# One matmul adds masks and the negative maximum to attention scores, in place of a second query tile and selects on GpSimd

## The chip, the cores and the metric

The kernel runs on one core of a Trainium2 chip. The metric is the device time of one execution in microseconds (us). The runs of the kernel before give 1493.66, 1497.61 and 1716.20 us; the median is 1497.61 us.

## The reference

Two layers of a decoder trunk are computed for a prompt of 1024 tokens and for 8 samples of 4 new tokens each, which share the weights. Layer 0 is attention: one input projection gives queries, keys and values for type A (a window of 128, with a sink logit in the denominator) and for three dilated groups of type B, 8 query heads over 2 key heads of width 64 each; then a gate, an output projection and a layer norm. Layer 1 is an mLSTM. The change touches the prompt's attention in layer 0, whose core is this (queries in blocks of 128 read their own and the block of keys before):

```python
def banded_attention(q, k, v, span, sink=None):
    ...
    s = jnp.einsum('nbqhgd,nbkhd->nbhgqk', qb, kk, preferred_element_type=F32)
    dist = qi - ki
    band = (dist >= 0) & (dist <= span)
    ...
    p, den, lse = _softmax_stats(s, mask, sink_b)
    o = jnp.einsum('nbhgqk,nbkhd->nbqhgd', p, vv.astype(F32))

def _softmax_stats(s, mask, sink):
    s = jnp.where(mask, s, NEG_INF)
    m = s.max(-1)
    ...
    p = jnp.exp(s - m[..., None])
    den = p.sum(-1)
```

The samples attend to their caches of 128, 128, 512 and 2048 rows (the last two strided, 128 rows of each taken).

## The kernel before

Layer 0 projects keys and values (`proj_kv`), then queries of four groups (`proj_q`, g = 0 for type A, 1 to 3 for type B with strides 1, 4, 16) and the gate (`proj_z0`), all through weights split into a high and a low part. Queries, keys and values go to DRAM scratch (QQ, KK, VV) and come back per group and key head (`kv`).

Attention has two passes. `stats` finds each query's maximum with masked scores in the layout queries x keys; `neg_rows` turns the maxima into rows of -maximum and stores them as a 129th row of QQ. `scores` (line 450) then computes the scores again in the layout keys x queries, for 4 heads x 128 queries at a time: a query block (`qb`). A query block has one score block (own keys) or two (the block before as well), as `blocks` says: 15 for each kv in groups 0 and 1, 12 in group 2, 8 in group 3, 100 in all. A score block is

- two matmuls into a PSUM tile `sc`: K1 (high keys twice, 128 rows) times Q1 (high and low queries), and K2 (low keys and a row of ones, 65 rows) times Q2 (high queries and the row of -maximum),
- `p = exp(sc)` on ScalarE (L465),
- the mask: selects on GpSimd that write zeros into `p` (L468 to L476),
- `ph`, `p` rounded, on ScalarE (`hi`, L112), and `pl = p - ph` on VectorE (`lo`, L116), or on GpSimd for every fourth block of type B (L481),
- three matmuls of `ph`, `ph` and `pl` with the values into `av` (L485 to L487), which VectorE adds to the outputs OD (L578, L580).

`q2_load` (line 364) makes Q2 for two query blocks at a time: one DMA of the -maximum row (1 partition x 4 x 256) and a copy of Q1's high half on ScalarE (L370). `k_load` makes K1 and K2, with a memset of the row of ones.

The order of the work is set in two steps. `weave` interleaves streams by planned costs: type A and the statistics of groups 1 and 2 with the projections of queries; then the statistics of group 3 and the scores of groups 3, 2, 1 for kv = 0, and the start of those for kv = 1, with the gate projections; then the rest of kv = 1 (`self.late`), the attention of the samples (`sample_attn`) and merges into the mixed activations (`merge0`). The framework's scheduler then puts every engine's instructions into one order by a model of their times, and each engine runs its own in that order. Nearly all DMAs are issued by SyncE (`load`, L106, and `store`, L109), in order too.

`sample_attn` loads the caches' keys and values into tiles KT (`sample_keys`, from a pool `smt` of 4 buffers that is opened after the pool `sm` is released at line 970), multiplies them (sS at L681, so at L728), and is followed in `out0` by the output projection (py, L165 to L167), whose weights (wr <- in_wo0) come through two buffers.

## Time and profile before

| | |
|---|---|
| median of the runs | 1497.61 us |
| profiled execution | 1500.81 us |
| its span, first to last instruction | 1499.1 us |
| mean granted clock of TensorE | 0.973 |
| TensorE busy (matmul) | 1405.4 us, 94% |
| VectorE busy | 901.5 us, 60% |
| ScalarE busy | 515.1 us, 34% |
| GpSimd busy | 276.0 us, 18% |

The profile is of one execution. Its engines are PE (TensorE matmul), PEld (its weight loads), DVE (VectorE), ACT (ScalarE), POOL (GpSimd) and SP (SyncE, which issues DMAs); an L number is a line of the kernel. Busy shares are means over stages with different limits, so a stage is read by its own stretch of time. Type A's scores run from 192 to 345 us, those of groups 3, 2 and 1 from 467 to 636 us, layer 0's output projection to 800 us, and layer 1 after that.

### The profile page before, as it was taken

The numbers are of one execution on the slowest core, as the hardware profiler recorded it, in microseconds if no ns is written. First come the engines' busy times: TensorE is split into PE (matmuls) and PEld (weight loads), VectorE is DVE, ScalarE is ACT, GpSimd is POOL, SyncE is SP. The second block draws the span as 40 slices with busy tenths as digits, with TensorE's granted clock in tenths as the row PEclk, the third lists the DMA queues.
The fourth block names the chain that finished last, engine by engine and source line by source line (L and its number), as shares of the span: only waits on it lengthen the run. The fifth ranks groups of instructions, "written<-read, shape, count | busy, mean of one in ns | idle before, by whom it ended". The sixth has DMA issues, their size and how long they took to land.

```text
span 1499.1 us, 21984 instructions
## 1 busy us (share of the span) xinstructions
PE 1405.4 (94%) x7792; PEld 1191.7 (79%) x7792; DVE 901.5 (60%) x2479; ACT 515.1 (34%) x938; POOL 276.0 (18%) x351
## 2 busy tenths in 40 slices
PE   8999999998899778979999999999999999999997
PEld 7989999898898444458788878988898899877785
DVE  5411457578566858768764536655565565566786
ACT  5332244542123776621133313331333133333310
POOL 1002233422322866401000000100000000000010
PEclk9999999999999888989999999999999999999999
DMA  8445655556653766794212655354223312431731
GB/s 307 168 142 171 199 190 164 173 162 185 186 190 111 195 169 186 241 300 140 95 51 87 220 191 201 109 194 124 78 82 122 108 50 69 131 116 39 233 131 46
DMA packets 139307, 226.86 MB, mean 151 GB/s; under 512 B 17216, under 2 KB 107296, under 8 KB 138680
## 3 DMA queue, kind: packets, MB, share of 16 engines
q1 hardware_dynamic: 131134, 204.09, 44.5%
q10 hardware_dynamic: 8064, 21.37, 4.0%
q8 instruction: 62, 1.02, 0.3%
q14 instruction: 47, 0.39, 0.1%
HBM read 166.60 MB, written 81.88 MB: 166 GB/s over the span
## 4 chain that ended last, share of the span: by engine, by line
PE 69%; DMA 16%; DVE 8%; issue 3%; ACT 2%; POOL 2%; SPq 1%; DVEq 0%; ACTq 0%; POOLq 0%
PE pj L199 10%; PE pj L201 10%; PE pj L200 10%; PE py L165 4%; PE py L167 3%; PE py L166 3%; DMA G<-GR 3%; PE pvo L165 3%; PE pvo L166 3%; PE pvo L167 3%; DMA wr<-in_wo_dram 1%; PE st L433 1%; DMA QZ<-QQ 1%; DMA out_cmems_dram<-Cs 1%; PE sc L463 1%
## 5 line engine op out<-in xcount | busy, mean ns | idle before, releaser
L199 PE MATMUL pj<-xh,wh 128*128 128x384 f32 (+1 forms) x576 | 189.3, 329 | 8.1 <-DVE sz L613 3.6
L199 PE MATMUL pj<-x1h,wh 128*128 128x384 f32 (+1 forms) x576 | 189.5, 329 | 1.7 <-ACT QT L1152 1.6
L200 PE MATMUL pj<-xl,wh 128*128 128x384 f32 (+1 forms) x576 | 188.5, 327 | 0.0
L201 PE MATMUL pj<-xh,wl 128*128 128x384 f32 (+1 forms) x576 | 188.4, 327 | 0.0
L201 PE MATMUL pj<-x1h,wl 128*128 128x384 f32 (+1 forms) x576 | 187.6, 326 | 0.0
L200 PE MATMUL pj<-x1l,wh 128*128 128x384 f32 (+1 forms) x576 | 187.4, 325 | 0.0
L199 PEld LDWEIGHTS pj<-xh,wh 128*128 128x128 f32 x576 | 110.6, 192 | 12.7 <-DVE sz L613 4.5
L199 PEld LDWEIGHTS pj<-x1h,wh 128*128 128x128 f32 x576 | 108.5, 188 | 6.5 <-issue 3.3
L201 PEld LDWEIGHTS pj<-x1h,wl 128*128 128x128 f32 x576 | 108.4, 188 | 6.0 <-issue 5.8
L200 PEld LDWEIGHTS pj<-xl,wh 128*128 128x128 f32 x576 | 110.5, 192 | 1.6
L201 PEld LDWEIGHTS pj<-xh,wl 128*128 128x128 f32 x576 | 110.8, 192 | 1.1
L200 PEld LDWEIGHTS pj<-x1l,wh 128*128 128x128 f32 x576 | 108.5, 188 | 4.0 <-issue 3.8
L437 DVE CUSTOM_DVE_ANT_0 junk<-st,maskq 128x256 f32<-128x256 f32 (+1 forms) x256 | 93.1, 364 | 27.4 <-PE st L433 6.8
L165 PE MATMUL pvo<-voh,x1h 128*128 128x512 f32 x256 | 101.0, 397 | 2.6 <-DVE SZ L1168 2.6
L166 PE MATMUL pvo<-voh,x1l 128*128 128x512 f32 x256 | 100.3, 394 | 0.0
L167 PE MATMUL pvo<-vol,x1h 128*128 128x512 f32 x256 | 99.7, 393 | 0.0
L807 POOL TENSOR_TENSOR rsw<-rsw,mhalf 128x1 f32<-128x1 f32 (+1 forms) x54 | 40.0, 741 | 322.3 <-DVE rsw L806 306.6
L116 DVE TENSOR_TENSOR pl<-p,ph 128x512 fp32r<-128x512 f32 x82 | 67.0, 825 | 29.0 <-ACT ph L112 27.0
L122 POOL TENSOR_TENSOR wl<-wr,wh 128x1024 fp32r<-128x1024 f32 x24 | 57.9, 2414 | 130.1 <-ACT qs L233 69.9
L112 ACT ACTIVATE wh<-wr 128x1024 fp32r<-128x1024 f32 x48 | 50.7, 1056 | 73.9 <-PE pj L200 69.6
L112 ACT ACTIVATE ph<-p 128x512 fp32r<-128x512 f32 x100 | 60.7, 627 | 27.0 <-POOL p L474 9.3
L1198 POOL MEMSET V<- 128x2 f32 x64 | 4.3, 99 | 348.6 <-PE num L1327 213.9
(350 smaller groups left out, 3244.8 us busy)
## 6 DMA issues: line engine op xcount, KB each, us to landing
Q<-QQ SPq DMA_DIRECT2D x32, 512.0 KB
out_kvs_dram<-in_cache_b_kv_dram SPq DMA_DIRECT2D x16, 1022.0 KB
wr<-in_w0f_dram SPq DMA_DIRECT2D x24, 512.0 KB
wr<-in_w1f_dram SPq DMA_DIRECT2D x24, 512.0 KB
QQ<-sh ACTq DMA_DIRECT2D x16, 512.0 KB
QQ<-sl ACTq DMA_DIRECT2D x16, 512.0 KB
QZ<-QQ SPq DMA_DIRECT2D x32, 256.0 KB
wr<-in_wo_dram SPq DMA_DIRECT2D x16, 512.0 KB
```

The lines of the kernel that those rows point to most:

```text
L112: return self.nc.scalar.activation(out, in_, AF.Copy, scale=scale)
L116: return self.nc.vector.tensor_tensor(out, in_, f(hi), OP.subtract)
L122: self.nc.gpsimd.tensor_tensor(out, in_, f(hi), OP.subtract)
L165: nc.tensor.matmul(ps, xh[:, k, t], wh, start=k == 0, stop=False)
L166: nc.tensor.matmul(ps, xl[:, k, t], wh, start=False, stop=False)
L167: nc.tensor.matmul(ps, xh[:, k, t], wl, start=False, stop=k == 7)
L199: nc.tensor.matmul(ps[:, :n], wh[:, k, :], xh[:, k, :n], start=k == 0, stop=False)
L200: nc.tensor.matmul(ps[:, :n], wh[:, k, :], xl[:, k, :n], start=False, stop=False)
L201: nc.tensor.matmul(ps[:, :n], wl[:, k, :], xh[:, k, :n], start=False, stop=k == 7)
L433: nc.tensor.matmul(st[:, u, :], Q1[:, h, q0:q0 + 128], K1[:, w0:w0 + 256], start=True, stop=True)
L437: nc.vector.tensor_tensor_reduce(junk[:, :n], st[:, u, c0:c0 + n], mk, 1.0, -3e38, OP.add, OP.max, ST[:, 8 * h + qb:8 * h + qb + 1])
L807: nc.gpsimd.tensor_tensor(r, v, self.mhalf[:m], OP.pow)
```

## The change

The row of -maximum and the mask come from one matmul of their own. Its weights `maskm` hold, for each of 127 queries of the block, that query's mask over the 128 keys (0 or -1e30), and in row 127 ones; its moving tile `E` holds in rows 0 to 126 the one-hot rows of those queries (the one query of 128 whose mask is empty needs none: the last for own keys, the first for the block before) and in row 127 the -maximum of 4 heads x 128 queries. Group 3, whose block is two strides of 64 queries, takes two such matmuls of half the width. So there are three matmuls to `sc` for two (four in group 3), and Q2 and its copy are gone: K2, now 128 rows with zeros in the lower half and kept in two fixed tiles KZ, multiplies Q1. The selects on GpSimd are gone. The exponential is computed twice from `sc`, once into `ph` and once into `p` (`p` has 3 buffers for 4). `mask_load` fills row 127 of one of two fixed tiles EM for every query block, by two DMAs of 1 x 4 x 128, one for each of the tile's two sets of one-hot rows. EM, KZ and `maskm` are tiles of the pool `sm`.

```diff
@@ -361,22 +361,16 @@
         self.store("Qh", f(Q[0:64]), self.QQ[g].rearrange("(d h) t -> d h t", h=8)[0:64, h, t])
         return Q
 
-    def q2_load(self, g, kv, hf, Q1):
-
-        Q2 = self.qp.tile([65, 4, 256], F32R, tag="Q2", name="Q2")
-        t = slice(256 * hf, 256 * hf + 256)
-        h = slice(4 * kv, 4 * kv + 4)
-        self.load(f(Q2[64:65]), self.QQ[g].rearrange("(d h) t -> d h t", h=8)[128:129, h, t])
-        self.nc.scalar.activation(Q2[0:64], f(Q1[0:64]), AF.Copy)
-        return Q2
-
     def k_load(self, g, kv, low=True):
...
         dil = DIL[g]
         src = self.KK.rearrange("(d h) t -> h d t", h=8)[2 * g + kv]
         K1 = self.kp.tile([128, TP], F32R, tag="K1", name="K1")
-        K2 = self.kp.tile([65, TP], F32R, tag="K2", name="K2") if low else None
+        K2 = None
+        if low:
+            K2 = self.KZ[self.nk % 2]
+            self.nk += 1
         if dil == 1:
             self.load(f(K1[0:64]), src[0:64])
             if low:
@@ -389,8 +383,6 @@
                 nc.vector.tensor_copy(d.rearrange("p (r n) -> p n r", r=dil),
                                       kt[64 * u:64 * u + 64].rearrange("p (n r) -> p n r", r=dil))
         nc.scalar.activation(K1[64:128], f(K1[0:64]), AF.Copy)
-        if low:
-            nc.gpsimd.memset(f(K2[64:65]), 1.0)
         return K1, K2
 
     def v_load(self, g, kv):
@@ -447,11 +439,32 @@
         nc.scalar.activation(NM, tr[:32, :128], AF.Copy, scale=-1.0)
         self.store('m', dst.rearrange("h (b q) -> (h b) q", q=128), f(NM))
 
-    def scores(self, g, kv, hf, Q1, Q2, K1, K2, V, emit):
+    def mask_load(self, g, kv, qb):
+
+        E = self.EM[self.ne % 2]
+        self.ne += 1
+        r = self.QQ[g][1024 + 4 * kv:1028 + 4 * kv, 128 * qb:128 * qb + 128]
+        for u in range(2):
+            self.load(f(E[127:128, u]), r.unsqueeze(0))
+        return E
+
+    def mask(self, g, kind, E, so):
+
+        nc = self.nc
+        if g == 3:
+            for u in range(2):
+                q = slice(64 * u, 64 * u + 64)
+                nc.tensor.matmul(so[:, :, q], self.maskm[:, 2 + u, :], E[:, u, :, q], start=False, stop=False,
+                                 skip_group_check=True)
+        else:
+            nc.tensor.matmul(so, self.maskm[:, kind, :], E[:, kind], start=False, stop=False)
+
+    def scores(self, g, kv, hf, Q1, K1, K2, V, emit):
         nc = self.nc
         for qb in range(2 * hf, 2 * hf + 2):
             q0 = 128 * (qb % 2)
             bl = self.blocks(g, qb)
+            E = self.mask_load(g, kv, qb)
             sct, avt = self.bps
             av = self.pp.tile([66, 512], F32, tag=avt[qb % len(avt)], name="av")
             for bi, (kb, kind) in enumerate(bl):
@@ -460,23 +473,13 @@
                 ks = slice(128 * kb, 128 * kb + 128)
                 so = sc.rearrange("p (h q) -> p h q", h=4)
                 nc.tensor.matmul(so, K1[:, ks], Q1[:, :, q0:q0 + 128], start=True, stop=False)
-                nc.tensor.matmul(so, K2[:, ks], Q2[:, :, q0:q0 + 128], start=False, stop=True)
-                p = self.ppool.tile([128, 512], F32, tag="p", name="p", bufs=4)
-                nc.scalar.activation(p, sc, AF.Exp)
-                if g == 3:
-                    pv = p.rearrange("p (h s q) -> p h s q", h=4, s=2)
-                    nc.gpsimd.affine_select(pv[:, :, 0, :], pv[:, :, 0, :], [[0, 4], [1, 64]], OP.is_ge, 0.0,
-                                            base=0, channel_multiplier=-1)
-                    nc.gpsimd.affine_select(pv[:, :, 1, :], pv[:, :, 1, :], [[0, 4], [1, 64]], OP.is_ge, 0.0,
-                                            base=64, channel_multiplier=-1)
-                    nc.gpsimd.memset(pv[0:64, :, 1, :], 0.0)
-                elif kind == 0:
-                    nc.gpsimd.affine_select(p, p, [[0, 4], [1, 128]], OP.is_ge, 0.0, base=0, channel_multiplier=-1)
-                else:
-                    nc.gpsimd.affine_select(p, p, [[0, 4], [-1, 128]], OP.is_ge, 0.0, base=0, channel_multiplier=1)
+                self.mask(g, kind, E, so)
+                nc.tensor.matmul(so, K2[:, ks], Q1[:, :, q0:q0 + 128], start=False, stop=True)
+                p = self.ppool.tile([128, 512], F32, tag="p", name="p")
                 ph = self.ppool.tile([128, 512], F32R, tag="ph", name="ph")
                 pl = self.ppool.tile([128, 512], F32R, tag="pl", name="pl")
-                self.hi(ph, p)
+                nc.scalar.activation(ph, sc, AF.Exp)
+                nc.scalar.activation(p, sc, AF.Exp)
                 if g and self.nsc % POOL_LO == 0:
                     nc.gpsimd.tensor_tensor(pl, p, f(ph), OP.subtract)
                 else:
@@ -532,8 +535,7 @@
 
         for hf in range(4):
             Q1 = self.q1_load(0, kv, hf)
-            Q2 = self.q2_load(0, kv, hf, Q1)
-            yield from self.scores(0, kv, hf, Q1, Q2, K1, K2, V, emit)
+            yield from self.scores(0, kv, hf, Q1, K1, K2, V, emit)
         self.store('o', self.OD[0][kv], OD)
         self.finish(0, kv, nm)
 
@@ -586,8 +588,7 @@
 
             for hf in range(4):
                 Q1 = self.q1_load(g, kv, hf)
-                Q2 = self.q2_load(g, kv, hf, Q1)
-                yield from self.scores(g, kv, hf, Q1, Q2, K1, K2, V, emit)
+                yield from self.scores(g, kv, hf, Q1, K1, K2, V, emit)
         if kv == 0:
             self.finish(1, kv)
 
@@ -920,6 +921,19 @@
             self.QZ = [sm.tile([128, 4, 256], F32R, name=f"QZ{u}") for u in range(2)]
             for Q in self.QZ:
                 nc.gpsimd.memset(f(Q[64:128]), 0.0)
+
+            self.nk = self.ne = 0
+            self.KZ = [sm.tile([128, TP], F32R, name=f"KZ{u}") for u in range(2)]
+            for K in self.KZ:
+                nc.gpsimd.memset(f(K[64:128]), 0.0)
+            raw = self.wraw.tile([128, 1024], F32, tag="wraw", name="mkr")
+            self.load(raw[:, 0:640], A['maskm'])
+            self.maskm = sm.tile([128, 4, 128], F32R, name="maskm")
+            self.hi(self.maskm, raw[:, 0:512].rearrange("p (u k) -> p u k", u=4))
+            self.EM = [sm.tile([128, 2, 4, 128], F32R, name=f"EM{u}") for u in range(2)]
+            for E in self.EM:
+                for u, e in enumerate((self.ident, raw[:, 512:640])):
+                    nc.vector.tensor_copy(E[:, u], e.unsqueeze(1).to_broadcast([128, 4, 128]))
             run(self.proj_q(0))
             self.done = 0
             self.bps = AB_PS[0]
@@ -1568,6 +1582,12 @@
     own2 = np.where((k <= q) & (k // 64 == q // 64), 0, NEG)
     mq = np.concatenate([prev, own, own2], 1)
     d['maskq'] = mq.astype(np.float32)
+
+    one = np.ones((1, 128))
+    half = np.zeros((63, 128))
+    mm = [own[:127], prev[:0:-1], own2[:64], own2[:63:-1]]
+    mm = [np.concatenate([m, half[:127 - len(m)], one], 0) for m in mm]
+    d['maskm'] = np.concatenate(mm + [np.eye(128)[::-1]], 1).astype(np.float32)
     row = np.arange(128)
     tt = (row % 4)[:, None]
     kk, nn = np.arange(128)[None], np.arange(32)[None]
```

The scheduler lays the whole program out anew. Three places show what stands in the new order.

SyncE, where the loads for the first scores of group 3 begin (kt and wr are key and weight loads, Q1 and Q2 query tiles, EM0 and EM1 the two tiles E, QQ3 the group's scratch). Before:

```order
L106 DMA Q2_4185<-QQ3_78 1x4x256
L106 DMA Q2_4254<-QQ3_78 1x4x256
L106 DMA wr_6575<-in_wo0_dram 128x1024 [waits Pool_49]
L106 DMA kt_5205<-KK_80 128x1024 [waits DVE_49]
L106 DMA Q1_4341<-QQ3_78 128x4x256 [waits DMAHW5_49,PE_49]
L106 DMA Q2_4343<-QQ3_78 1x4x256 [waits DMAHW7_49,DMAHW1_49,PE_49]
L106 DMA Q1_4410<-QQ3_78 128x4x256 [waits DMAHW0_49,PE_49,Activation_49]
L109 DMA NMB12_88<-NM_4156 32x128 [waits Activation_49]
L106 DMA Q2_4412<-QQ3_78 1x4x256 [waits DMAHW2_49,PE_49]
```

Now:

```order
L106 DMA EM0_962<-QQ3_78 1x4x128 [waits DMAHW3_49]
L106 DMA EM0_962<-QQ3_78 1x4x128
L106 DMA EM1_963<-QQ3_78 1x4x128
L106 DMA EM1_963<-QQ3_78 1x4x128 [waits DMAHW7_49]
L106 DMA kt_5220<-KK_80 128x1024 [waits DVE_49]
L106 DMA EM1_963<-QQ3_78 1x4x128 [waits DMAHW6_49,DMAHW1_49,PE_49]
L106 DMA EM1_963<-QQ3_78 1x4x128 [waits DMAHW7_49,DMAHW2_49,PE_49]
L106 DMA EM0_962<-QQ3_78 1x4x128 [waits DMAHW3_49,PE_49]
L106 DMA EM0_962<-QQ3_78 1x4x128 [waits DMAHW5_49,DMAHW4_49,PE_49]
L106 DMA Q1_4355<-QQ3_78 128x4x256 [waits PE_49]
```

One load of a row for two query blocks has become four, and from the third query block on each waits for TensorE (PE) to be done with the tile.

SyncE, where the samples' loads begin (KT <- in_kt0, in_vc0; mf, mo: loads of the merges; QQ1: group 1, the last of the scores). Before:

```order
L106 DMA Q1_5863<-QQ2_77 128x4x256 [waits DMAHW0_49,PE_49]
L106 DMA Q2_5865<-QQ2_77 1x4x256 [waits DMAHW2_49,PE_49]
L109 DMA FD10_95<-dn_5198 32x128 [waits DVE_49]
L106 DMA KT_5795<-in_kt0_dram 128x512 [waits DMAHW7_49,DMAHW3_49,DMAHW2_49]
L106 DMA KT_5851<-in_kt0_dram 128x512 [waits DMAHW4_49]
L106 DMA KT_5900<-in_vc0_dram 128x512 [waits DMAHW5_49]
L106 DMA KT_5935<-in_vc0_dram 128x512 [waits DMAHW6_49]
L106 DMA mf_5972<-FD10_95 64x2x384
```

Now:

```order
L106 DMA EM1_963<-QQ1_76 1x4x128 [waits DMAHW4_49,PE_49]
L106 DMA mo_6146<-OD11_92 64x2x384 [waits DMAHW3_49,DMAHW0_49,Pool_49]
L106 DMA EM1_963<-QQ1_76 1x4x128 [waits DMAHW5_49,PE_49]
L106 DMA mf_6147<-OD11_92 64x2x384
L106 DMA mo_6146<-OD11_92 64x2x384 [waits DMAHW6_49]
L106 DMA mf_6147<-OD11_92 64x2x384 [waits DMAHW7_49]
L106 DMA KT_5804<-in_kt0_dram 128x512 [waits DMAHW2_49,DMAHW4_49,DMAHW1_49,PE_49]
L106 DMA KT_5861<-in_kt0_dram 128x512
L106 DMA KT_5909<-in_vc0_dram 128x512
```

Before, the samples' loads stand between loads for group 2 and wait for no engine; now they stand behind the last row load of group 1 and wait for TensorE.

TensorE, at the first score of the samples (sS; sc and av are the prompt's scores and outputs). Before:

```order
L462 MATMUL sc_5809<-Q1_5803,K1_5471 128x512 [waits DMAHW3_49,Activation_49]
L463 MATMUL sc_5809<-Q2_5805,K2_5472 128x512 [waits DMAHW4_49]
L485 MATMUL av_5425<-ph_5434,V_5211 66x512 [waits DVE_49,PE_49]
L486 MATMUL av_5425<-ph_5434,V_5211 64x512
L487 MATMUL av_5425<-pl_5435,V_5211 66x512
L681 MATMUL sS_5797<-KT_5795,scrh_5734 32x128 [waits DMAHW7_49,DMAHW3_49,DMAHW2_49]
L681 MATMUL sS_5797<-KT_5795,scrh_5734 32x128 x3
L462 MATMUL sc_5824<-Q1_5803,K1_5471 128x512 [waits Activation_49]
L463 MATMUL sc_5824<-Q2_5805,K2_5472 128x512
L681 MATMUL sS_5853<-KT_5851,scrh_5734 32x128 [waits DMAHW4_49]
```

Now:

```order
L475 MATMUL sc_6406<-Q1_6351,K1_6031 128x512 [waits PE_49,Activation_49]
L460 MATMUL sc_6406<-EM1_963,maskm_960 128x512 [waits DMAHW4_49]
L477 MATMUL sc_6406<-Q1_6351,KZ1_955 128x512
L488 MATMUL av_6392<-ph_6398,V_6035 66x512 [waits Activation_49]
L489 MATMUL av_6392<-ph_6398,V_6035 64x512
L682 MATMUL sS_5806<-KT_5804,scrh_5741 32x128 [waits DMAHW0_49,PE_49]
L682 MATMUL sS_5806<-KT_5804,scrh_5741 32x128 x3
L682 MATMUL sS_5863<-KT_5861,scrh_5741 32x128 [waits DMAHW1_49]
L682 MATMUL sS_5863<-KT_5861,scrh_5741 32x128 x3
L490 MATMUL av_6355<-pl_6375,V_6035 66x512 [waits DVE_49]
```

Before, sS stands among the score blocks of group 2 (the tiles made from kt), with many to follow; now the first stands behind the last score block's matmuls (sc_6406).

## Rows read from the trace of the kernel before

**Rows 1.** The page, the chain that ended last, by engine.

```profile
PE 69%; DMA 16%; DVE 8%; issue 3%; ACT 2%; POOL 2%; SPq 1%; DVEq 0%; ACTq 0%; POOLq 0%
```

**Rows 2.** Stretches: busy us of PE, PEld, DVE, ACT, POOL; PEclk; DMA; GB/s.

```profile
192.00:345.00 153.00, 148.40 (x869) 137.16 (x868) 97.15 (x241) 72.99 (x119) 56.57 (x48) 0.99 0.54 167
...
489.00:560.00 71.00, 54.48 (x178) 30.36 (x177) 51.23 (x70) 52.95 (x87) 53.63 (x66) 0.83 0.67 182
560.00:636.00 76.00, 64.66 (x290) 31.43 (x289) 60.27 (x107) 49.85 (x98) 43.93 (x52) 0.89 0.72 220
636.00:670.00 34.00, 23.39 (x201) 17.05 (x200) 20.13 (x23) 9.38 (x12) 1.84 (x1) 0.90 0.97 300
```

**Rows 3.** The same for L463 alone: PE, PEld; PEclk; DMA; GB/s.

```profile
192.00:345.00 153.00, 11.56 (x30) 5.62 (x30) 0.99 0.54 167
465.00:489.00 24.00, 3.70 (x10) 1.80 (x10) 1.00 0.38 124
489.00:636.00 147.00, 25.81 (x60) 12.83 (x60) 0.86 0.70 201
```

**Rows 4.** 489 to 636 us: xcount | busy, mean ns | idle; pl: min/median/max.

```profile
L112 ACT ACTIVATE ph<-p 128x512 fp32r<-128x512 f32 x66 | 39.8, 624 | 20.0 <-POOL p L474 8.5 <-POOL p L472 5.5 <-PE av L486 4.0
L116 DVE TENSOR_TENSOR pl<-p,ph 128x512 fp32r<-128x512 f32 x49 | 37.6, 775 | 11.9 <-ACT ph L112 10.1 <-PE av L487 1.8
L465 ACT ACTIVATE p<-sc 128x512 f32<-128x512 f32 x64 | 36.3, 587 | 8.2 <-PE sc L463 4.1 <-POOL pl L481 2.3 <-DVE pl L116 1.7
...
L474 POOL TENSOR_SCALAR_AFFINE_SELECT p<-p 128x512 f32<-128x512 f32 x32 | 29.4, 923 | 13.5 <-ACT p L465 13.4
...
L370 ACT ACTIVATE Q<-Q 64x1024 fp32r<-64x1024 f32 x19 | 20.0, 1051 | 10.7 <-DMA Q<-QQ 10.7
...
L690 DVE SCALAR_TENSOR_TENSOR scrl<-sS,scrh,scrl 128x128 f32<-128x128 f32 x12 | 4.2, 349 | 0.2
...
L116 DVE TENSOR_TENSOR pl<-p,ph x49: 615/692/1527, 491.9 to 633.5; 128x512 fp32r<-128x512 f32 x49
```

**Rows 5.** TensorE's waits from 489 to 636 us: total, times, longest.

```profile
PE av L485 <- ACT ph L112: 8.6, 6, 4.2
```

**Rows 6.** Two of TensorE's matmuls in order of time: start, us.

```profile
643.00 0.39 PE L166 MATMUL py<-oh,ml 128*128 128x512 f32 x1
643.23 0.40 PE L167 MATMUL py<-ol,mh 128*128 128x512 f32 x1
```

**Rows 7.** DMA issues of L106, 489 to 640 us: ns min/median/max, first and last.

```profile
L106 SPq DMA_DIRECT2D Q<-QQ x38: 359/562/1046, 488.8 to 610.7; - x38
L106 SPq DMA_DIRECT2D KT<-in_kt_dram x12: 328/346/588, 572.8 to 608.5; - x12
```

**Rows 8.** DMAs in the chain: start, us to landing.

```profile
458.32 1.71 DMA QQ<-nr
...
475.34 5.76 DMA NMB<-NM
...
542.61 6.08 DMA Q<-QQ
...
595.72 4.31 DMA KT<-in_kt_dram
```

**Rows 9.** DMA issues of the samples' keys and values: count, size.

```profile
KT<-in_kt_dram SPq DMA_DIRECT2D x8, 512.0 KB
KT<-in_vc_dram SPq DMA_DIRECT2D x8, 512.0 KB
...
KT<-in_kt_dram SPq DMA_DIRECT2D x4, 256.0 KB
KT<-in_vc_dram SPq DMA_DIRECT2D x4, 256.0 KB
```

**Rows 10.** SyncE in order of time, samples' values: start, us of issue.

```profile
639.82 2.10 SPq L106 DMA_DIRECT2D KT<-in_vc_dram  x2
...
645.75 0.90 SPq L106 DMA_DIRECT2D KT<-in_vc_dram  x2
```

## The prediction

> **What bounds the kernel now.** I read the page's chain first: TensorE holds 69% of the work that ended last, GpSimd 2% [rows 1]. So work taken from GpSimd counts only where TensorE waits for it, and work given to TensorE counts wherever TensorE is full. The table by stretches says where that is [rows 2]. From 192 to 345 us (attention A woven with projections) TensorE is busy 148.4 of 153 us at a granted clock of 0.99: full. From 489 to 636 us (the score blocks of groups 3, 2, 1 for both KV halves, the last 60 of the 100) it is busy 54.5 + 64.7 = 119 of 147 us, at 0.83 and 0.89. From 636 to 670 us DMA is at 0.97 of its engines' time and 300 GB/s: that stretch, in which the end of sample attention, the merges and the first weights of the output projection come in, is bound by transfers. All 100 blocks are in the first two stretches and the projections between them [rows 3].
>
> In the second stretch no engine is full. VectorE has 51.2 + 60.3 = 111.5 us of 147, ScalarE 102.8, GpSimd 97.6 [rows 2]. The list of instructions there [rows 4] shows the chain of a block: exponential 0.587 us on ScalarE, select 0.923 us on GpSimd, copy to `ph` 0.624 us on ScalarE, subtraction 0.775 us on VectorE or, every fourth, on GpSimd. ScalarE idles 8.5 us in front of `ph` for the select of L474 and 5.5 us for the memset of L472; the list of waits shows what arrives at TensorE of it: 8.6 us for `ph`, the longest of the waits [rows 5].
>
> **The change part by part.**
>
> *Matmuls.* Each block gains one matmul, each of the 16 blocks of group 3 two of half the width: 84 + 32 = 116. Its row shows 0.39 us, but that is latency: one starts 0.23 us after the other [rows 6]. 116 x 0.23 = 27 us of TensorE work, the half-width ones counted in full. The third matmul now uses 128 rows for 65, which changes no columns. In attention A 30 x 0.23 = 7 us fall on a full engine, with nothing to hide behind: +7. The other 20 us fall into the second stretch.
>
> *The block chain.* Select, memset and the dependence of `ph` on `p` go. The second exponential replaces the copy: 0.587 for 0.624 us, so nothing gained or lost on ScalarE; the 32 copies of Q2 (19 of them here, 20.0 us [rows 4]) are a gain to ScalarE, and GpSimd loses most of its 97.6 us. What is late next: TensorE's own work for 60 blocks is 60 x 6 x 0.23 = 83 us and 3 us for the extra halves, 86 in all. VectorE keeps subtractions, accumulation and merges; from its 111.5 us goes the vector work of the sample scores, which leave this stretch (below), about 12 us by my estimate (its largest group is 4.2 us [rows 4]), and some 4 us of subtraction: with the selects gone I let the mean of `pl`, 0.775 us, fall to its median, 0.692 us, 49 times [rows 4]. So VectorE at 95 us is the fullest. Now it is busy 0.76 of the stretch; with the chain two steps shorter I take 0.8, so 95 / 0.8 = 119, say 120 us instead of 147: -27. The bounds: 95 us (VectorE back to back, -52), and above, the queue of loads (next), 156 us (+9).
>
> A rule bears on the subtraction. The trace shows `pl` from 0.615 to 1.527 us on VectorE [rows 4]. The Trainium skill (SBUF — State Buffer, section "SBUF: two separate sides") says that a VectorE operation with two SBUF inputs and a GpSimd operation exclude each other at one port pair for a whole instruction; that would make the long ones waits for a select, and the fall to the median sure. Were the spread from elsewhere, VectorE would keep the 4 us, 99 us in place of 95 in the bound below.
>
> *The row loads.* Before, 32 loads of 4 KB (one for two query blocks); now 128 of 2 KB, two for each query block, into two buffers. SyncE takes a median 0.562 us to issue one of the loads of Q [rows 7], so 1.1 us for a query block. A buffer is free when the mask matmul of its query block is done, and wanted two query blocks later. A pair of query blocks can therefore not be faster than 1.1 us of issue + the landing L of the second + 0.23 us for the mask, and 6 x 0.23 = 1.4 us more where a query block has two score blocks and holds its buffer through both. Landings in the chain: 1.71 us for a 16 KB row store alone, 5.76 us for another, 6.08 us for the 512 KB of Q1 that such a load may stand behind [rows 8]. Of the 48 query blocks of the three groups the first 10 (group 3 but for a few, one block each) came ahead of 489 us [rows 3]; the other 38 are 19 pairs, 15 of them with a query block of two: 19 L + 19 x 1.33 + 15 x 1.4 = 19 L + 46, so 79 us at 1.71 and 156 us at 5.76. The loads decide from L = 3.9 us on, where this reaches 120 us. I take the short landing, since 8.4 MB leave this stretch (below), and say that the loads are hidden.
>
> On small loads the Trainium skill (DMA: Bandwidth & Descriptors, section "Rules for kernel authors") says to coalesce, since under 64 KB one pays mostly overhead; these are 2 KB each, so it speaks against the change. The trace agrees for the quiet case (1.71 us for 16 KB); the 5.76 us beside it is more than overhead. By the quiet landing the sum stays, by the other it is the first rival.
>
> *The sample attention.* This is what the diff does not say. The new buffers live in the pool that is released ahead of the sample tiles, and are used until the last score block. In the new order of SyncE the first loads of sample keys stand behind the last row loads and wait for TensorE, and TensorE's first sample scores come behind the last score matmul. Before, the first such load went out at 572.8 us, 63 us ahead of the end of the scores [rows 7]. The loads are 16 x 512 KB and 8 x 256 KB, 10.5 MB [rows 9]; only four, 2.1 MB, were issued after 636 us [rows 10]. So 8.4 MB move behind the scores into a stretch that is bound by transfers: 8.4 MB at 300 GB/s = 28 us. To this I add two landings of 4.31 us [rows 8], one after the last score and one where four buffers turn around between keys and values: 28 + 8 = +36. From below: merges and weights use the gaps, and a quarter of the second stretch's transfers are gone, so they can come earlier: 14 us. From above, with no overlap between batches of four buffers: 55 us.
>
> *Setup.* One load, one copy, four vector copies and memsets stand beside 100 us of projections on a full TensorE: nothing; a few us if the load's buffer delays a weight tile.
>
> *Sum.* +7 - 27 + 36 = +16 us on the profiled execution's 1500.81 us (span 1499.1, 1.7 us around it), which is 3.2 us above the median of the runs, 1497.61. On the median: 1514 us, +1.1%. About 2% (30 us) is what a measurement of this kernel can tell from no change, so this is inside it. Own range: 1498 to 1528.
>
> **The rivals.**
>
> *The row loads become the bound* (slower). Place: TensorE in front of each mask matmul, from a landing of 3.9 us on. For it: SyncE's queue is in order, a row load waits there for TensorE and holds what stands behind it, and Q1's 512 KB take up to 6.08 us. Against it: the sample loads are gone from this stretch. At landings of 4.4 to 5.8 us the 19 pairs take 130 to 156 us: -17 to +9 in place of -27. With 7 + 36: +26 to +52, middle 1537 us.
>
> *Scores at the bound of an engine* (faster). The chain gets so short that VectorE runs back to back, 95 us (-52), and the transfers behind cost the lower 14 to 27 us, as fewer compete: 7 - 52 + 20 = -25, 1473 us. For it: GpSimd's and ScalarE's loads fall, TensorE's clock of 0.83 to 0.89 would rise with fuller work. Against it: no engine in that stretch is above 0.76 now.
>
> *The selects were not what the stretch waits for*, so the change doesn't do what it says. TensorE's named waits for `ph` are 8.6 us [rows 5]; the rest is accumulation, Q and order. Then only 9 of the 27 us come: 7 - 9 + 36 = +34, 1532 us.
>
> **How the numbers follow.** Forecast 0.50, loads bound 0.24, engine bound 0.14, selects beside the point 0.12. Slower by over 2% (above 1527.6): 0.05 of the forecast's half, 0.17 and 0.09 of the two slower rivals: 0.31. Faster by over 2% (below 1467.7): 0.07 of the engine rival and 0.01: 0.08. Same: 0.61. The range goes from near the engine rival, 1480, to the upper end of the loads rival, 1550.
>
> **What would show it.** Right: `ph` no longer waits for GpSimd; the last score block ends near 616 us (636 + 7 - 27); the first sample key load goes out after it; from there DMA near 300 GB/s and TensorE mostly idle for 50 us and more; first full output projection near 685 us. Wrong: waits of TensorE on the row loads of several tens of us (loads rival); a score stretch under 105 us (engine rival); sample loads out ahead of the last scores, or the output projection starting within 25 us of them, which would break the +36.

## The result, and the profile after

The changed kernel takes 1536.1 us (median of 4 runs, 1534.4 to 1543.2) beside 1497.3 us before: ratio 1.0277, 95% interval 1.0232 to 1.0322. The ratio is one of means, without the run of 1716.20 us, which was in a slower state of the chip. It is slower by 2.8%; forecast was +1.1%, no change. The profiled execution took 1543.16 us (span 1541.4), the longest of the four, and 42.3 us more of span than before.

The page's chain by engine, after; beside [rows 1] TensorE and "issue" have one point more, DMA, VectorE and GpSimd one less:

```profile
PE 70%; DMA 15%; DVE 7%; issue 4%; ACT 2%; POOL 1%; SPq 1%; DVEq 0%; ACTq 0%; POOLq 0%
```

The stretches of [rows 2], after, and one behind them (busy us of PE, PEld, DVE, ACT, POOL; PEclk; DMA; GB/s):

```profile
192.00:345.00 153.00, 150.73 (x868) 137.42 (x868) 88.87 (x220) 62.19 (x110) 31.33 (x17) 1.00 0.50 158
...
489.00:560.00 71.00, 59.18 (x231) 37.49 (x231) 51.24 (x73) 43.11 (x80) 15.41 (x14) 0.93 0.60 176
560.00:636.00 76.00, 58.80 (x247) 37.02 (x251) 51.22 (x77) 39.39 (x76) 14.65 (x11) 0.86 0.58 164
636.00:670.00 34.00, 14.78 (x68) 2.88 (x56) 22.61 (x43) 3.19 (x6) 1.80 (x1) 0.55 0.84 258
670.00:690.00 20.00, 15.31 (x140) 9.24 (x140) 4.76 (x11) 4.33 (x17) 1.26 (x1) 0.59 0.62 210
```

GpSimd's load fell from 97.6 to 30.1 us between 489 and 636 us, as meant. But from 636 to 670 us TensorE is busy 14.8 of 34 us where it had 23.4, and its granted clock is 0.55 where it was 0.90.

Where the 42 us came from is read off the first and last start of a few matmuls: `st` (statistics: the first one ends the setup, the last one attention A and the projections woven into it), the last of the values, `av<-pl`, and the last of the output projection, `py<-ol`. TensorE's instructions on these tiles (ns min/median/max, first to last start in us), of the kernel before:

```profile
L433 PE MATMUL st<-K,QZ x256: 276/282/552, 173.4 to 468.7; 128*128 128x256 f32 x128
...
L487 PE MATMUL av<-pl,V x100: 387/396/694, 208.9 to 635.6; 128*66 128x512 f32 x100
...
L167 PE MATMUL py<-ol,mh x128: 387/389/796, 640.3 to 760.8; 128*128 128x512 f32 x128
```

and after:

```profile
L425 PE MATMUL st<-K,QZ x256: 277/281/467, 180.0 to 481.9; 128*128 128x256 f32 x128
...
L490 PE MATMUL av<-pl,V x100: 387/393/694, 217.0 to 630.1; 128*66 128x512 f32 x100
...
L167 PE MATMUL py<-ol,mh x128: 387/389/628, 697.1 to 804.7; 128*128 128x512 f32 x128
```

From these starts I take four stages for every kernel: setup (to the first `st`), A (first to last `st`), B (last `st` to last `av<-pl`), and the tail (from there to the last `py`). The rest of the program is 735 to 738 us in all of them. A stage ends with an instruction, and the scheduler can move other work over that border: behind the last `st` stand 86 matmuls of the query projections (`pj`) in the kernel before, e2 and e5, and 35 or 36 in the others of the table.

| us, one profiled execution each | setup | A | B | tail | B + tail |
|---|---|---|---|---|---|
| before | 173.4 | 295.3 | 166.9 | 125.2 | 292.1 |
| after | 180.0 | 301.9 | 148.2 | 174.6 | 322.8 |
| e1, own pool | 179.2 | 298.5 | 163.4 | 135.4 | 298.8 |
| e2, before with K2 held | 172.1 | 290.9 | 156.4 | 167.4 | 323.8 |
| e3, copies on GpSimd | 171.2 | 300.9 | 150.6 | 173.0 | 323.6 |
| e4, e1 and e3 | 171.9 | 301.7 | 157.6 | 135.5 | 293.1 |
| e5, e4 with A as before | 171.8 | 291.5 | 163.7 | 128.2 | 291.9 |
| e8, e4 without B's masks | 173.2 | 297.8 | 142.3 | 135.4 | 277.7 |
| f3, after, one sample load | 178.1 | 300.0 | 147.8 | 170.9 | 318.7 |
| f4, after, sample scores twice | 177.5 | 300.9 | 147.5 | 182.7 | 330.2 |

After minus before: setup +6.6, A +6.6, B -18.7, tail +49.4, rest -1.6, in sum +42.3.

The setup's 6.6 us stand in the chain of waits after (start, us):

```profile
111.44 7.11 DMA KVN<-KV
118.86 1.02 DVE EM L936
120.00 3.60 DVE EM L936 x3
123.59 0.47 DVE sl L117
124.11 0.69 PE pj L199
```

The four copies that fill the one-hot tiles stand in VectorE's queue ahead of `sl`, the low part of the projected queries. `sl` reads a projection's sums, the PSUM tile `pj`; TensorE, whose next matmul writes to `pj`, waits for `sl`, 5.5 us in one piece.

In B the wait of [rows 5] is gone but for 1.3 us. TensorE's waits from 489 to 636 us, after (total, times, longest):

```profile
PE av L490 <- DVE pl L116: 6.8, 4, 3.4
PE sc L475 <- DMA Q<-QQ: 6.3, 5, 2.0
PE sc L457 <- DMA EM<-QQ: 6.3, 7, 1.8
...
PE av L488 <- ACT ph L481: 1.3, 1, 1.3
```

The exponentials now wait for TensorE and no longer the other way round; the same stretch by line, beside [rows 4]:

```profile
L481 ACT ACTIVATE ph<-sc 128x512 fp32r<-128x512 f32 x68 | 40.9, 602 | 43.2 <-PE sc L477 30.1 <-PE av L489 12.1 <-DVE pl L116 0.6
L116 DVE TENSOR_TENSOR pl<-p,ph 128x512 fp32r<-128x512 f32 x51 | 35.8, 708 | 11.0 <-ACT p L482 9.2 <-PE av L490 1.6
```

In the tail TensorE waits for everybody a little; its waits from 620 to 710 us:

```profile
PE pT L709 <- ACT scrl L700: 11.6, 2, 9.0
PE sS L682 <- DMA KT<-in_kt_dram: 7.2, 3, 4.5
PE py L165 <- ACT oh L112: 5.7, 2, 5.2
PE sS L682 <- DVE scrl L689: 5.0, 2, 4.5
...
PE so L724 <- ACT scrl L712: 1.7, 2, 1.2
```

and the samples' first load goes out at 620.3 us, where [rows 7] has 572.8:

```profile
L106 SPq DMA_DIRECT2D KT<-in_kt_dram x12: 327/372/982, 620.3 to 650.2; - x12
```

The samples' score matmuls with 512 columns take nearly twice as long; before, then after:

```profile
L681 PE MATMUL sS<-KT,scrl x32: 589/593/617, 600.2 to 619.1; 128*32 128x512 f32 x32
```

```profile
L682 PE MATMUL sS<-KT,scrl x32: 1030/1060/1063, 643.6 to 660.3; 128*32 128x512 f32 x32
```

### The profile page after: what moved, and what is told of

Its sections match the earlier page's. It is cut to its first block, busy times and chain, and to the rows that moved or that the text cites. A ratio compares the mean times of both kernels' runs of the same rounds, so it can differ in the third digit from the quotient of the medians.

```text
span 1541.4 us, 22195 instructions
## 1 busy us (share of the span) xinstructions
PE 1431.8 (93%) x7908; PEld 1216.0 (79%) x7908; DVE 894.1 (58%) x2483; ACT 482.0 (31%) x907; POOL 173.9 (11%) x213
## 3 DMA queue, kind: packets, MB, share of 16 engines
q8 instruction: 63, 1.03, 0.3%
## 4 chain that ended last, share of the span: by engine, by line
PE 70%; DMA 15%; DVE 7%; issue 4%; ACT 2%; POOL 1%; SPq 1%; DVEq 0%; ACTq 0%; POOLq 0%
PE pj L199 10%; PE pj L200 10%; PE pj L201 10%; PE py L165 4%; PE py L166 4%; PE py L167 3%; PE pvo L165 3%; PE pvo L166 3%; PE pvo L167 3%; DMA G<-GR 2%; DMA QZ<-QQ 2%; DMA wr<-in_wo_dram 1%; PE av L488 1%; PE sc L475 1%; PE av L489 1%
## 5 line engine op out<-in xcount | busy, mean ns | idle before, releaser
L481 ACT ACTIVATE ph<-sc 128x512 fp32r<-128x512 f32 x100 | 60.1, 602 | 76.8 <-PE sc L477 60.5
L116 DVE TENSOR_TENSOR pl<-p,ph 128x512 fp32r<-128x512 f32 x82 | 59.9, 737 | 20.0 <-ACT p L482 18.1
L425 PE MATMUL st<-K,QZ 128*128 128x256 f32 x256 | 51.7, 289 | 9.7 <-DMA QZ<-QQ 4.9
```

The costliest lines, as they stand in the source:

```text
L116: return self.nc.vector.tensor_tensor(out, in_, f(hi), OP.subtract)
L425: nc.tensor.matmul(st[:, u, :], Q1[:, h, q0:q0 + 128], K1[:, w0:w0 + 256], start=True, stop=True)
L481: nc.scalar.activation(ph, sc, AF.Exp)
```

## The experiments

Theory: the loss is not in the new matmuls of attention B but in the memory of their tiles, which holds the sample attention back to the end of the scores, and beside it in the setup's copies and the masks of attention A. Rivals: transfers and the clock in the tail, the row loads, the second exponential. Every ratio is to runs of the kernel before on the same chip.

**e1: the fixed tiles in a pool of their own.**

```diff
-                tc.tile_pool(name="odp", bufs=1) as self.odp:
+                tc.tile_pool(name="odp", bufs=1) as self.odp, tc.tile_pool(name="kzp", bufs=1) as kz:
...
-            self.KZ = [sm.tile(
+            self.KZ = [kz.tile(
...
-            self.maskm = sm.tile(
+            self.maskm = kz.tile(
...
-            self.EM = [sm.tile(
+            self.EM = [kz.tile(
```

> The changed kernel with the key operands, the mask operands and the one-hot tiles in a pool of their own, which is not released before the sample tiles are taken. Theory A (the loss is the sample attention held back by the memory of these tiles): the first sample keys are issued tens of us before the last score matmul again, the output projection ends near 760 us instead of 803.8, and the kernel takes 1536 - 49 = 1487 us or so (1482 to 1498). Rival B (the loss comes from the sample's transfers and the low TensorE clock, wherever they stand): with the loads beside the scores, the row loads and the exponentials wait for them and the output projection still ends past 785 us, 1515 us or more.

Measured: 1514.8 us, ratio 1.0138 (1.0111 to 1.0165), 21 us less than the changed kernel's 1.0277. The samples' loads and the end of the projection:

```profile
L106 SPq DMA_DIRECT2D KT<-in_kt_dram x12: 327/432/587, 567.7 to 606.1; - x12
...
L167 PE MATMUL py<-ol,mh x128: 387/389/793, 657.2 to 776.5; 128*128 128x512 f32 x128
```

The loads are back before the last scores and the tail is 39 us shorter, as theory A has it; but B is 15 us longer, so only half of the 49 us come back. So the place is theory A's, and the time is not: 1514.8 us lies above its 1482 to 1498 and at the edge of its rival's 1515, and the projection ends between the two forecasts. With the samples between them, the scores take 15.2 us longer than without; in the kernel before that was 10.5 us (before against e2).

**e2: the kernel before, with K2 alone held in `sm`.**

```diff
-        K2 = self.kp.tile([65, TP], F32R, tag="K2", name="K2") if low else None
+        K2 = None
+        if low:
+            K2 = self.K2s[self.nk % 2]
+            self.nk += 1
...
+            self.K2s = [sm.tile([65, TP], F32R, name=f"K2s{u}") for u in range(2)]
+            for K in self.K2s:
+                nc.gpsimd.memset(f(K[64:65]), 1.0)
```

> The kernel before with one thing of the change alone: the second key operand is two fixed tiles of the pool that is released before the sample attention (its row of ones set once), everything else as it was. Theory A: the first sample keys wait for the last score matmul (623 us), the output projection ends 36 to 49 us later than 760 us, and the kernel takes 1533 to 1546 us though no matmul is added. Rival B: within 8 us of 1497 us. Rival C (the memsets of ones that go from GpSimd set its pace): below 1490 us.

Measured: 1531.9 us, ratio 1.0240 (1.0208 to 1.0272). No matmul, no row load, no second exponential, and still 35 us slower, 1 us under theory A's range:

```profile
L106 SPq DMA_DIRECT2D KT<-in_kt_dram x12: 327/330/617, 606.5 to 657.5; - x12
...
L488 PE MATMUL av<-pl,V x100: 387/396/692, 207.6 to 619.4; 128*66 128x512 f32 x100
...
L167 PE MATMUL py<-ol,mh x128: 387/392/775, 633.5 to 786.8; 128*128 128x512 f32 x128
```

The loads go out right behind the last score matmul (605.4 us). The tail is 42 us longer than before and B 10.5 us shorter, with nothing changed there but K2's tiles and their memsets. B and tail together are 324 us, as in the changed kernel (323). This shows the main cause by itself: the held memory. It doesn't show what fills the tail, since the layout is another one: in e2 the projection's first matmuls stand between the samples' steps from 629.2 us on, its weight loads begin at 633.2 us, and DMA is at 1.03 of its engines' time and 308 GB/s from 636 to 670 us. Its profiled execution is also the shortest of its four, 7 us below their median, and the end of the projection, 26 us later than before, falls short of the 36 to 49 of theory A.

**e3: the one-hot tiles filled by GpSimd.** **e4: e1 and e3 together.**

```diff
-                    nc.vector.tensor_copy(E[:, u], e.unsqueeze(1).to_broadcast([128, 4, 128]))
+                    nc.gpsimd.tensor_copy(E[:, u], e.unsqueeze(1).to_broadcast([128, 4, 128]))
```

> The changed kernel with the four copies that fill the one-hot tiles on GpSimd instead of VectorE. Theory A (these copies, queued on VectorE ahead of the low parts of the query projection's weights, cost the 6.6 us by which the first statistics matmul is late): the first st matmul is back at 173 to 175 us and the kernel takes 1529 to 1531 us. Rival B (the load of the mask matrices, not the copies, holds the stage): first st matmul still near 180 us, 1536 us. Rival C (the copies now hold GpSimd's own low parts of weights): later than 180 us, 1538 us or more.

> Both edits at once. Theory A: the gains add, 1487 - 6 = 1481 us or so (1476 to 1492), which is faster than the kernel before by some 1%. Rival B: not below 1510 us.

Measured: e3 1533.3 us, ratio 1.0253 (1.0224 to 1.0281); e4 1504.6 us, 1.0070 (1.0047 to 1.0093). The first `st` stands at 171.2 us in e3, 8.8 us earlier than after, but the runs give back only 4 us of it, with intervals that overlap; from e1 to e4 it is 10 us. So the copies cost some 4 to 10 us. Between e3's theories (1529 to 1531 us, 1536 us) the time is undecided, its mark is theory A's. e4 misses theory A's 1476 to 1492 us by 13: its B + tail is back at 293.1 us, but its A is still 301.7.

**e5: attention A as before.** In e4, `scores` of attention A takes a Q2 again (in the memory of EM, which is filled behind attention A), with selects, one exponential and a copy.

```diff
-                self.mask(g, kind, E, so)
-                nc.tensor.matmul(so, K2[:, ks], Q1[:, :, q0:q0 + 128], start=False, stop=True)
+                if Q2 is None:
+                    self.mask(g, kind, E, so)
+                    nc.tensor.matmul(so, K2[:, ks], Q1[:, :, q0:q0 + 128], start=False, stop=True)
+                else:
+                    nc.tensor.matmul(so, K2[0:65, ks], Q2[:, :, q0:q0 + 128], start=False, stop=True)
```

> e4 with attention A computed as in the kernel before (a second query tile with the row of -maximum, no mask matmul, selects on GpSimd, one exponential and a copy); attention B as in the changed kernel. The kernel e4 takes 1.007 of the kernel before, its A takes 301.7 us from the first statistics matmul to the last against 295.3 us before. Theory A (the masks of attention A are pure addition, since TensorE bounds that stage): the stage is back at 295 us and the ratio goes down by 6 us to 1.003 (1.001 to 1.005). Rival B (the stage gains from the removed selects and copies as much as it pays): ratio 1.006 to 1.009.

Measured: 1496.2 us, ratio 0.9985 (0.9959 to 1.0011): 0.0085 or 13 us below e4, and no longer apart from the kernel before. This misses both theories: A gave 6 us by the one and next to none by the other. A takes 291.5 us, 10.2 less than in e4; but there are also 50 projection matmuls fewer in it, which stand behind the last `st` instead. With pool, copies and attention A undone the whole loss is gone, and attention B with its masks on TensorE is worth nothing either way: B + tail 291.9 us against 292.1. That the last 13 us are due to A's masks is not shown: e7, below, keeps them all and is as fast.

**e6: no row loads. e7: one exponential. e8: no masks in B.** All from e4.

```diff
...
-        for u in range(2):
-            self.load(f(E[127:128, u]), r.unsqueeze(0))
```

```diff
-                nc.scalar.activation(ph, sc, AF.Exp)
                 nc.scalar.activation(p, sc, AF.Exp)
+                self.hi(ph, p)
```

```diff
-                self.mask(g, kind, E, so)
+                if g == 0:
+                    self.mask(g, kind, E, so)
```

> e4 without the loads of -maximum into row 127 of the one-hot tiles (the rows keep what they were filled with, so the maximum isn't subtracted; everything else is issued as in e4). Theory A (the row loads cost little more than the 4.7 us that TensorE shows waiting for them): 3 to 6 us less than e4, 1.003 to 1.005. Rival B (two issues for each of 48 query blocks hold SyncE and the loads behind them, up to the sample keys and the merges): 12 us less or more, ratio below 0.999.

> e4 with one exponential and a copy of it (p from the scores, ph a copy of p) in place of two exponentials of the scores. Theory A (ScalarE has room, busy 82 us of the 147 us from 489 to 636, so the form of the second operation hardly counts): within 3 us of e4, ratio 1.005 to 1.009. Rival B (what the second exponential brings is the shorter way from scores to values: ph no longer waits for p): the values wait some 0.6 us more per block where TensorE is short of work, 6 to 15 us slower than e4, ratio 1.011 to 1.017.

> e4 without the mask matmuls of attention B (the 54 whole ones and 32 halves; the row loads stay, nothing is masked there and the maximum isn't subtracted). Theory A (with the selects gone TensorE bounds the score stretch: it is busy 127 us of the 147 from 489 to 636): the 54 x 0.23 + 32 x 0.12 = 16 us come off nearly whole, 10 to 16 us less than e4, ratio 0.996 to 1.000. Rival B (VectorE bounds it, as the forecast had it): 0 to 4 us less, ratio 1.004 to 1.007.

Measured: e6 1.0026 (0.9992 to 1.0059), 7 us below e4 by the ratios, 4 by the medians, with intervals that overlap: about theory A's 3 to 6, and short of the 12 of its rival. e8 0.9931 (0.9906 to 0.9956), 21 us below e4 in the runs and 15.3 us in B alone, for 16 us of matmuls: TensorE bounds attention B once it carries the masks. (The 6.4 us that TensorE waits for row loads in B of e4 go with them, and its waits for Q1 grow from 4.4 to 12.0 us, so the 15 us are the price of the masks with their loads.) Its mark, the stage ends 15 us earlier:

```profile
L491 PE MATMUL av<-pl,V x100: 387/393/678, 208.6 to 613.3; 128*66 128x512 f32 x100
```

e7 missed both theories: 0.9992 (0.9966 to 1.0017), 12 us faster than e4, though the second operation is the same work. Three of the next four runs follow that up.

**e9: e5 with one exponential. e10: the changed kernel with one exponential. e12: e4 with one exponential in A alone. e11: e9 with `POOL_LO = 3`.** The edit is that of e7, in e12 under `if g == 0`.

> e5 (attention A as in the kernel before, own pool, one-hot tiles filled by GpSimd) with one exponential and a copy in attention B too: of the change only the masks of attention B by matmul stay. e5 stands at 0.9985 of the kernel before, e7 (one exponential everywhere, masks in both attentions) at 0.9992 against 1.007 for e4. Theory A (the 8 us by which e7 beats e4 are a property of one exponential in attention B and the tail): the two gains add, ratio 0.989 to 0.994. Theory B (they came in attention A, which e7 ran in 295.3 us and e4 in 301.7, or from where the instructions came to stand): no gain left over e5, ratio 0.996 to 1.001.

> The changed kernel with one exponential and a copy, and nothing else altered (one-hot tiles, keys and masks still in the pool that the sample attention waits for). Theory A (two exponentials cost 8 us whatever the rest): 8 us below the changed kernel, ratio 1.016 to 1.023. Theory B (the 8 us of e7 depended on its order of instructions): ratio 1.025 to 1.031.

> e4 with one exponential and a copy in attention A alone, two exponentials in attention B. Theory A (the gain of e7 belongs to attention B and the tail): ratio as e4, 1.005 to 1.009. Theory B (it belongs to attention A): near e7, 0.998 to 1.002.

> e9 with every third instead of every fourth low part of the probabilities of attention B on GpSimd, which the selects have left. Theory A (TensorE bounds the score stretch of attention B once the masks are matmuls): within 4 us of e9. Rival (VectorE bounds it, at 0.71 to 1.4 us for each low part): some 6 low parts fewer on VectorE, 4 us less or more.

Measured: e9 0.9999 (0.9981 to 1.0018), no gain over e5 (theory B); e10 1.0227 (1.0201 to 1.0254), 7.5 us below the changed kernel, inside theory A, though its interval overlaps that of the changed kernel; e12 1.0028 (1.0008 to 1.0049), between e4 and e7 and outside both theories; e11 0.9981 (0.9963 to 0.9999), 3 us below e9, within theory A. So a second exponential brings nothing. By the ratios it costs 6 us in attention A (e12 against e4) and in attention B between nothing (e9 against e5) and 5 us (e7 against e12). Why is open: the scheduler lays out the whole program anew for every such edit, and these runs can't part that from the operation. The traces show how much it moves. Behind the last `st` stand 36 projection matmuls in e4 and 89 in e7, e10 and e12; A takes 301.7 us in e4, and 294.4 to 296.1 in the three kernels with all of A's masks and one exponential there (e7, e10, e12), against 295.3 before. In the profiled executions of e12 and e4 the 5.6 us that A is shorter come back in B + tail (300.6 us against 293.1). No version that does the whole work was clearly faster than the kernel before: e11's 3 us are the best.

**f3: one load in place of the samples' 24. f4: the samples' scores twice.** Both from the changed kernel, to settle what the tail is made of.

```diff
-        out = []
+        t = self.kt0
         if g < 2:
-            t = st.tile([128, 4, 128], F32, tag="KT", name="KT")
-            self.load(t, src[:, 4 * a:4 * a + 4])
-            return [t[:, j:j + 1] for j in range(4)]
...
+            return [t[:, 0, j:j + 1] for j in range(4)]
+        return [t[:, 0], t[:, 1]] * 2
...
+        self.kt0 = st.tile([128, 2, 4, 128], F32, tag="KT", name="KT")
+        self.load(self.kt0, self.A['kt'][2][:, 0:2])
```

```diff
-            for j in range(4):
+            for j in (0, 1, 2, 3, 0, 1, 2, 3):
                 nc.tensor.matmul(S[32 * j:32 * j + 32, :w], self.sQ[g][:, 4 * a + j, :],
...
```

> The changed kernel with one load in place of the 24 loads of sample keys and values (every sample step reads the same tile, so the samples' results are others; all matmuls, exponentials and sums stay). The tail from the last value matmul to the last output projection takes 173.7 us in the changed kernel and 125.2 in the kernel before. Theory A (the transfers set the pace of the held-back sample attention, as the forecast's 28 us had it): 20 us less or more, ratio at most 1.014. Theory B (the chain of matmul, VectorE, ScalarE and transpose at a granted clock of 0.50 to 0.66 sets it, the transfers lie beside it): less than 8 us less, ratio 1.022 or more. Between the two, both share in it.

> The changed kernel with each score matmul of the sample attention issued twice (the second writes what the first wrote): 8 steps of four more, at 1.06 us for one of 512 columns and 0.42 us for one of 128 in the changed kernel; four 512-column ones of one step overlap and take some 1.7 us at that clock, so 4 x 1.7 + 4 x 0.7 = 9 to 10 us. Theory A (transfers): hidden in the waits, ratio 1.026 to 1.030. Theory B (TensorE's part of the chain is on the path): 7 to 12 us more, ratio 1.032 to 1.036. Theory C (the low clock costs more than the matmuls): the clock rises above 0.66 and the kernel is no slower or faster, ratio below 1.026.

Measured: f3 1535.1 us, ratio 1.0259 (1.0214 to 1.0304). The 10 MB are gone, DMA falls from 0.84 to 0.35 between 636 and 670 us, and TensorE is no busier there:

```profile
636.00:670.00 34.00, 13.14 (x71) 4.00 (x72) 21.84 (x47) 7.15 (x21) 3.06 (x2) 0.55 0.35 90
```

The projection's first matmul starts 8.6 us sooner behind the last values (680.9 after 625.9 us, where it was 693.7 after 630.1), but its end only 3.7 us. TensorE's waits from 615 to 720 us have mostly changed their names. Of the 7.2 us for keys 3.4 are left, for the one load; VectorE's sums of scores (L682, L684, there L689, L691) and ScalarE's copies (L705, there L712) are waited for longer instead:

```profile
PE pT L702 <- ACT scrl L693: 11.7, 2, 9.1
PE py L165 <- ACT oh L112: 6.4, 3, 5.7
PE sS L675 <- DVE scrl L682: 5.2, 2, 4.7
PE sS L675 <- DVE scrl L684: 5.0, 2, 4.4
PE so L717 <- ACT scrl L705: 4.2, 2, 3.7
```

f4 1543.5 us, ratio 1.0328 (1.0289 to 1.0367), 8 us above the changed kernel by the ratios, with intervals that overlap, and its tail 8.1 us longer: the doubled matmuls are paid nearly in full (9 to 10 us were expected), most of them at the lower of the two clock levels (1.2 GHz of 2.4), which the granted clock of 0.50 from 630 to 636 us and 0.65 from there to 670 shows. The 512-column ones:

```profile
L682 PE MATMUL sS<-KT,scrl x64: 592/1061/1063, 640.3 to 657.9; 128*32 128x512 f32 x64
```

Both speak for theory B, in the changed kernel: the held-back sample attention is a chain of small steps over TensorE, VectorE and ScalarE, and the transfers lie mostly beside it.

## Why the prediction was wrong

*Right.* The place: sample loads behind the last scores (620.3 us, last `sc` at 619.9), the output projection near 685 (693.7, then 5.2 us in one wait for its weights). `ph` no longer waits for a select. The fall of `pl`: mean 775 to 708 ns, median 692 to 679. The Trainium skill (SBUF — State Buffer, section "SBUF: two separate sides") says that the port pair which VectorE and GpSimd share is held for a whole instruction. The fall agrees with it, though no run took the selects away alone, and single ones of 1.6 us remain. The row loads as rival: 6.3 us of waits in B, 4 to 7 us when taken away, so not the bound. On them the Trainium skill (DMA: Bandwidth & Descriptors, section "Rules for kernel authors") advises to coalesce small transfers. By e6 that could bring at most those 4 to 7 us.

*Right by number, not by reason: +7 for the masks in attention A.* A is 6.6 us longer. But from the first to the last `st` it holds 79 matmuls more (1755 for 1676): the 30 masks and 50 of the query projections (`pj`), which stood behind the last `st` before, less one `st` at the edge. The 50 are some 8 us of TensorE, an estimate from their starts (0.17 us apart for the 37 with 384 columns, 0.13 for the 13 with 288). And e7, e10 and e12, with the same masks, take 294.4 to 296.1 us for A, no longer than before. So the stage is longer by work from the next one, and the number came out by luck.

*Wrong, the term of +36 for the sample attention.* The step "8.4 MB at 300 GB/s = 28 us" put down to transfers what f3 shows to be a small part: without the loads the tail is 3.7 us shorter, no more. The sign named for it failed as well: DMA moved 258 and 210 GB/s from 636 to 690 us, not 300, and TensorE stood idle for 24 of these 54 us. The tail grew by 49.4 us: the projection starts 63.6 us behind the last values where it started 4.1 us behind them, and then takes 10.1 us less. What I had not priced is the chain itself: sums, exponentials, transposes and copies one after another, once the scores that used to fill the gaps are gone, and TensorE at a granted clock of 0.55 and 0.59 between 636 and 690 us, after a stretch with many gaps (from 620 to 630 us it was busy 3.5 of 10 us, at 0.76 after 1.00 in the 10 us before), where the 128x512 sample scores take 1.06 us against 0.593 before. What the clock alone costs is not shown: e2, at 0.95 from 636 to 670 us, has 7 us less tail, but also the projection between the samples' steps, and its profiled execution is at the short end of its runs where the changed kernel's is at the long end. Then the projection's weights, of which six of eight loads go out from 695.6 us on, stand behind the sample chain as well.

*Wrong, the term of -27 for the score stretch.* B fell by 18.7 us, and the last value matmul moved from 635.6 to 630.1 us, not to near 616. The step "VectorE at 95 us is the fullest" named the wrong engine. For TensorE it counted the blocks' matmuls alone, 86 us; but [rows 2] has it busy for 119 us, more than VectorE's 111.5, so that some 50 us of other work were left out, and "no engine in that stretch is above 0.76" was wrong by its own row (119 of 147 is 0.81). After the change TensorE had 118 of 147 us and VectorE 102.5, the exponentials waited 30.1 us for `sc`, and e8 gets 15.3 us out of B for 16 us of masks. Of the 18.7 us, 10.5 are the samples leaving (e2 has them without any change to the scores); the other 8.2 are about what the 50 projections moved into A are worth. So no gain of the blocks themselves is shown, and when the samples and the projections are back in their places, masks and selects weigh the same (e5).

*Wrong, setup at nothing.* The copies stood on VectorE ahead of the step that gives a full TensorE its PSUM tile back: +6.6 us, gone in e3 (first `st` at 171.2 us). The prediction looked at the load's buffer and a weight tile, and put nothing down for VectorE's queue.

Against the forecast's terms the tail came out 13.4 us dearer, the score stretch 8.3, the setup 6.6, attention A 0.4 and the rest 1.6 cheaper: 26.3 us, from +16 to +42.3. Of the rivals, the row loads' middle (1537 us) is nearest to the time by luck: its sign, waits of several tens of us for them, did not come. "The selects were not what the stretch waits for" (1532 us) is nearest to the reason: taking them away is worth no more than the masks cost.

## What to carry to other kernels

A tile that lives longer costs more than its instructions: ask of every new tile which pool's memory it holds, until when, and what starts in that memory next. Work that filled the gaps of another stage has a small price there (10.5 us here) and its full latency when it is left alone, so its cost was here its chain, not its bytes. Before moving work to an engine, look at what that engine has left in the stage, and count anew with the work that may come back to it.

## What was not expected

The same copy into the one-hot tiles took 1.22 to 1.25 us on VectorE and 0.61 to 0.62 us on GpSimd. The two from `ident`, in the changed kernel (ns min/median/max, first and last start):

```profile
L936 DVE CAST EM<-ident x2: 1218/1234/1250, 118.9 to 121.2; 128x512 fp32r<-128x512 f32 x2
```

and in e3:

```profile
L936 POOL CAST EM<-ident x2: 611/614/618, 121.9 to 123.0; 128x512 fp32r<-128x512 f32 x2
```

Spans on GpSimd are rough, and besides these only the two copies from the load were seen, with the same times. And computing an exponential twice was dearer by the ratios than computing it once and copying it in two pairs of kernels (e4 and e7, the changed one and e10) and not in a third (e5 and e9), for a reason that stays open.
